# A decoder trunk on one core: TensorE's order through the RWKV scan written out by hand, the small triangular solves moved to GpSimd, and unsplit fp32 weights in the prologue

## The chip, the core and the metric

The kernel runs on one core of a Trainium2 chip. The metric is the device time of one execution, in microseconds (us). TensorE (PE in the profile) does the matrix products, VectorE (DVE) and ScalarE (ACT) work on whole tiles, GpSimd (POOL) can do simple elementwise work, and SyncE (SP) issues DMAs. ACT issues DMAs too, from a queue of its own.

## What is computed

A two-layer decoder trunk over 272 tokens (16 learned ones and 256 given) of width 2048. Layer 0 is RWKV-7 time mixing and a SwiGLU; layer 1 is attention and a SwiGLU. The change is in the time mixing, whose heart is a recurrence over the tokens for 32 heads of 64:

```python
def step(state, inp):
    r_t, d_t, k_t, v_t, kk_t, a_t = inp
    sa = jnp.einsum('bhvk,bhk->bhv', state, -kk_t)
    state = (state * d_t[:, :, None, :]
             + sa[..., None] * (kk_t * a_t)[:, :, None, :]
             + v_t[..., None] * k_t[:, :, None, :])
    return state, jnp.einsum('bhvk,bhk->bhv', state, r_t)
...
y = ((y - mean) * lax.rsqrt(var + GN_EPS)).reshape(b, l, d) * gn_w + gn_b
bonus = (jnp.sum(rh * kh * r_k, axis=-1, keepdims=True) * vh).reshape(b, l, d)
out = ((y + bonus).astype(h.dtype) * g) @ w_o
```

Here r, k and v are projections of mixed neighbouring tokens with 2048 x 2048 weights, and decay, a and the gate g come from narrow two-factor projections (96 and 256 wide, called lora below).

## The kernel before

Activations lie transposed: 16 tiles (k) of 128 channels by 272 tokens. A **dense product** is one 128 x 128 weight block times one such tile. For fp32 accuracy at the faster fp32r rate each weight and activation is split into a high and a low part (ACT casts `whi`, DVE subtracts for `wlo`; the same with `hl` or `hi`/`lo` for activations), and `mm3k` issues three products a block (L191 to L193). So one output block of a projection is 16 x 3 = 48 dense products. A product in raw fp32 needs no split and shows as two records in the trace.

**Prologue** (`prologue`). Tokens are loaded, their squares summed on PE (`ss`), and `rstd_of` gives the norm (Ln, Exp, and four DVE steps, L575 to L578). The first three blocks of w_k are computed together, k outside, as the mixed tiles come (hn L452, u L428, xi L429, hl L254/255); `presplit` splits their weights (L421/422). Then the other 13 blocks follow. Between them the generator `rest` makes the first lora factors (`lr`, raw fp32, L497), g_w1 (split) and the other mixed activations. Each finished block gives the norm of its heads (`kq`, L469).

**Scan** (`pair`, one call for each of 16 pairs of heads). The 256 tokens are cut into 4 chunks of 64, the 16 first ones are a chunk of their own ("0"). A pair needs: zw and za (lora, three products each); v and r (48 dense products each); scaled operands (ARV, BK, AR0, B0, V0); bonus; score products `ba`, `bb` and `b`, masked on DVE into G; products z0 and k0 for chunk 0; transposes `tb` and `tv`, and `vc`, which centres v; the inverse of 40 unit triangular 16 x 16 blocks (**the solver**, L772 to L779, 29 steps on DVE, each of which needs the one before); its extension to 64 x 64 by `yb` and `zb`, twice (s = 16 and 32); `wa`, `rm`; then in bank `cb` the part of the states that needs no earlier state (L896), and four steps (L903), each of which needs S, copied and scaled by ACT from the step before (L905). Then group norm (`vb`), and the gate (`gp`). The solver's blocks go through DRAM to change layout: G is written to s1, the diagonal blocks come back as As, the result Ts goes to s2 and comes back as Tt. All these DMAs are issued on ACT.

What sets the order: pairs are generators, interleaved 13 yields apart (`STRIDE`), with `WAIT1` and `WAIT2` empty yields to cover DMAs; a scheduler then places each engine's instructions by its own estimate of when they are due. At the tail `wo_head` begins four blocks of w_o for 15 of their 16 input tiles (`KHEAD`); `wo_first` (L191 and so on) ends them. FFN and attention follow.

Of the kernel before, what the change touches and what calls it, by code (L numbers as in the profile page):

```python
# [11 lines left out]
F32 = mybir.dt.float32  # L12
# [13 lines left out]
HD = 64  # L26
# [14 lines left out]
L2B = {"da": 1, "g": 2}  # L41
# [3 lines left out]
NSQ = 4  # L45
RSTEP = 7
KR = 8
FRONT = {"zw", "za", "vc", "bonus", "ba", "bb", "z0", "k0", "b00", "b01"}
TAIL = {"wa", "rm0", "rm1", "cb", "vb", "gp"}
WAIT1 = 3  # L50
WAIT2 = 9
STRIDE = 13
PSTEP = 8
NHEAD = 4
KHEAD = 15
ASTRIDE = 2
ASTEP = 4
BUFS = {n: 2 for n in "ARV BK AR0 bv G An Tt pe X BV0 WV0".split()}


def _consts():
# [14 lines left out]
    put("blk", blk)  # L76
    put("blk64", blk / 64)
# [6 lines left out]
    put("mask3", np.concatenate([incl, strict, incl], 1))  # L84
# [20 lines left out]
    first = pos  # L105
    put("onesD", np.full((128, 128), 1.0 / D))
# [17 lines left out]
class Builder:  # L124
# [141 lines left out]
    def build(self):  # L266
        tc, nc = self.tc, self.nc
        with ExitStack() as ctx:
# [6 lines left out]
            nc.scalar.dma_start(self.vecs, self.a["vecs"])  # L275
            self.dvec = {"hdw0": 0, "ha0": NK, "oka": 2 * NK}
            self.dvec.update({f"om{i}": (3 + i) * NK for i in range(6)})
            self.dv = cp.tile([128, 9 * NK + 4], F32, name="dv")
            b = 9 * NK
            nc.vector.memset(self.dv[:, b:b + 1], RMS_EPS)  # L280
            nc.vector.memset(self.dv[:, b + 1:b + 2], GN_EPS)
            nc.vector.memset(self.dv[:, b + 2:b + 3], 1.0)
            self.eps = self.dv[:, b:b + 1]
            self.gneps = self.dv[:, b + 1:b + 2]
            self.one = self.dv[:, b + 2:b + 3]

            def v16(name):
                i = VEC.index(name) * NK
                return self.vecs[:, i:i + NK]

            for dst, src in (("hdw0", "dec_w0"), ("ha0", "a_w0")):
                o = self.dvec[dst]
                nc.vector.tensor_scalar(self.dv[:, o:o + NK], v16(src), 0.5, None, ALU.mult)
            nc.vector.tensor_scalar(self.dv[:, 2 * NK:3 * NK], v16("k_a"), -1.0, 1.0,
                                    ALU.mult, ALU.add)
            nc.vector.tensor_scalar(self.dv[:, 3 * NK:9 * NK], self.vecs[:, 0:6 * NK], -1.0, 1.0,
                                    ALU.mult, ALU.add)
            nv = len(VEC) * NK
            self.kgain = self.vecs[:, nv:nv + 1]
            self.qgain = self.dv[:, b + 3:b + 4]  # L300
            nc.vector.tensor_scalar(self.qgain, self.vecs[:, nv + 1:nv + 2], 128.0 ** -0.5, None,
                                    ALU.mult)
# [34 lines left out]

    def time_mix(self):
# [4 lines left out]
        self.xs2 = self.hid_ctx.enter_context(tc.tile_pool(name="xs2", bufs=2 * NK))  # L343
        self.kp = self.hid_ctx.enter_context(tc.tile_pool(name="kp", bufs=NK))
# [5 lines left out]
        self.fronts = 0  # L350
        with ExitStack() as ctx:
            sp = ctx.enter_context(tc.tile_pool(name="sp", bufs=1))
            self.l2 = ctx.enter_context(tc.tile_pool(name="l2", bufs=2))
# [3 lines left out]
            zero = sp.tile([128, 5, 65], F32, name="zero", tag="P")  # L357
            nc.gpsimd.memset(zero, 0.0)
            for i in range(2):
                st = {}  # L360
                for n, w in (("B0", 64), ("V0", 64), ("SC0", 128)):
# [5 lines left out]
                                  zero.rearrange("p a t -> p (a t)"))  # L367
                self.s2.append(z)
            self.interleave(lambda p: self.pair(p, sp), STRIDE, self.wo_head())
# [4 lines left out]
    def prologue(self, hid):  # L374
# [3 lines left out]
        with ExitStack() as ctx:  # L378
# [3 lines left out]
            hn = [self.xs2.tile([128, T + 1], F32, name="hn", tag="s") for _ in range(NK)]  # L382
            xx = [self.xs2.tile([128, T], F32, name="xx", tag="s") for _ in range(NK)]
            for k in range(NK):
                nc.sync.dma_start(xx[k], a["xT"][:, k, :])
# [14 lines left out]
            rstd = self.rstd_of(ss[:, :T])  # L400


            w0 = [[] for _ in range(G0)]
            raws = []
            n = 0

            def presplit(k0):
                nonlocal raws, n
                if k0 % 8 == 0:
                    raws = []  # L410
                    for m in range(G0):
                        raw = self.wraw.tile([128, 1024], F32, name="raw", tag="raw")
                        nc.sync.dma_start(raw, a["w_k"][m][:, k0 * 128:k0 * 128 + 1024])
                        raws.append(raw)
                for m in range(G0):
                    pool, t = (wx, ("w", "w")) if n < NWX // 2 else (self.whl, ("whi", "wlo"))
                    hi = pool.tile([128, 512], F32R, name="whi", tag=t[0])
                    lo = pool.tile([128, 512], F32R, name="wlo", tag=t[1])
                    n += 1
                    part = raws[m][:, k0 % 8 * 128:k0 % 8 * 128 + 512]  # L420
                    A.copy(hi, part)  # L421
                    V.tensor_tensor(lo, part, hi.bitcast(F32), ALU.subtract)
                    for k in range(4):
                        w0[m].append((hi[:, k * 128:k * 128 + 128], lo[:, k * 128:k * 128 + 128]))
# [21 lines left out]
            for k in range(NK):  # L446
                if k % 4 == 0:
                    presplit(k)
# [752 lines left out]
```

## Time and profile before

| | us |
|---|---|
| median of 3 runs (lowest, highest) | 2740.06 (2737.32, 2741.23) |
| the profiled execution; its span | 2741.77; 2740.0 |
| prologue: start to the scan's first product | 0 to 179.8 |
| scan, to the first dense product of wo_first | 179.8 to 683.2 |
| the rest: wo_first, FFN, attention, FFN | 683.2 to 2740.0 |

The granted TensorE clock was 0.995 over the span. In a row of instructions stand the source line, the engine, the operation, what it writes and reads, and its duration; in a row of groups the count, the busy time, the mean in ns, and the idle time of the engine just before with what ended it. Matmuls are pipelined, so the distance between two starts tells more than a duration.

### The profile page before, as it was taken

The page shows a single profiled execution, that of the slowest core. Times are in us where ns is not written, and L with a number is a line of the kernel's source. Part 1 is how long each engine was busy: PE and PEld are TensorE (multiplying, and loading weights), DVE is VectorE, ACT ScalarE, POOL GpSimd, SP SyncE. Part 2 cuts the span into 40 slices and gives each one's busy share as a digit, 9 for nine tenths or more (in the row PEclk, how much of TensorE's full clock was granted, in tenths as well). Part 3 has the DMA queues.
Part 4 walks back from the last instruction along what each step waited for, and adds up shares of the span by engine and source line. Part 5 has one row for each costly group of instructions (what it writes and reads, how often), then busy time and mean ns, then how long its engine had stood idle before and what let it go on. Part 6 is the DMA issues. An engine that isn't in the chain of part 4 may idle for free.

```text
span 2740.0 us, 53870 instructions
## 1 busy us (share of the span) xinstructions
PE 2689.3 (98%) x20862; PEld 2475.0 (90%) x20862; DVE 1864.8 (68%) x4176; ACT 1493.5 (55%) x3005; POOL 1.2 (0%) x11
## 2 busy tenths in 40 slices
PE   6999999998999999999999999999999999999999
PEld 5888888887999999999999999988888888888888
DVE  7677788786666555555556876577776666666665
ACT  6774555555554444444445764477555455454553
POOL 0000000000000000000000000000000000000000
PEclk9999999999999999999999999999999999999999
DMA  5443333332655555555555555533555665665655
GB/s 169 135 152 100 104 96 103 104 95 83 210 173 168 181 177 167 185 176 162 187 176 167 180 164 169 169 119 105 189 187 179 196 188 180 197 189 179 199 177 179
DMA packets 181279, 439.50 MB, mean 160 GB/s; under 512 B 57984, under 2 KB 84000, under 8 KB 181024
## 3 DMA queue, kind: packets, MB, share of 16 engines
q1 hardware_dynamic: 137632, 428.56, 49.4%
q10 hardware_dynamic: 43392, 7.52, 1.5%
q8 instruction: 163, 2.67, 0.4%
q14 instruction: 92, 0.75, 0.1%
HBM read 430.27 MB, written 5.74 MB: 159 GB/s over the span
## 4 chain that ended last, share of the span: by engine, by line
PE 91%; DVE 3%; DMA 3%; ACT 2%; ACTq 1%; issue 0%; SPq 0%; DVEq 0%
PE mm L197 22%; PE mm L191 16%; PE mm L193 16%; PE mm L192 15%; PE mm L196 11%; DMA raw<-w_k 1%; PE cb L903 1%; PE yb L831 1%; PE rm L871 1%; PE zb L848 1%; PE hms L1038 1%; PE cb L896 1%; PE z L1115 1%; DVE G L721 0%; PE ba L715 0%
## 5 line engine op out<-in xcount | busy, mean ns | idle before, releaser
L173 DVE TENSOR_TENSOR wlo<-raw,whi 128x512 fp32r<-128x512 f32 (+1 forms) x1596 | 1079.0, 679 | 622.3 <-ACT whi L172 598.7
L172 ACT CAST whi<-raw 128x512 fp32r<-128x512 f32 (+1 forms) x1596 | 967.6, 611 | 906.2 <-PE mm L192 577.0
L191 PE MATMUL mm<-hl,whi 128*128 128x272 f32 x3424 | 996.9, 292 | 19.4 <-ACT hl L254 18.5
L193 PE MATMUL mm<-hl,wlo 128*128 128x272 f32 x3424 | 995.9, 291 | 0.0
L192 PE MATMUL mm<-hl,whi 128*128 128x272 f32 x3424 | 991.4, 290 | 0.4 <-DVE hl L255 0.3
L197 PE MATMUL mm<-hl,whi 128*128 128x512 f32 x2624 | 919.8, 395 | 0.0
L196 PE MATMUL mm<-hl,wlo 128*128 128x256 f32 x2624 | 740.6, 282 | 0.0
L191 PEld LDWEIGHTS mm<-hl,whi 128*128 128x128 f32 x3424 | 645.8, 189 | 27.7 <-ACT hl L254 20.5
L192 PEld LDWEIGHTS mm<-hl,whi 128*128 128x128 f32 x3424 | 652.6, 191 | 4.2 <-DVE hl L255 1.3
L193 PEld LDWEIGHTS mm<-hl,wlo 128*128 128x128 f32 x3424 | 647.9, 189 | 4.8 <-issue 1.8
L197 PEld LDWEIGHTS mm<-hl,whi 128*128 128x128 f32 x2624 | 492.5, 188 | 112.7
L196 PEld LDWEIGHTS mm<-hl,wlo 128*128 128x128 f32 x2624 | 494.3, 188 | 0.6
L213 DVE TENSOR_TENSOR h<-h,mm 128x256 f32<-128x256 f32 (+1 forms) x224 | 93.9, 420 | 6.6 <-PE mm L197 6.0
L206 ACT COPY c<-mm 128x256 f32<-128x256 f32 x104 | 38.8, 373 | 79.0 <-PE mm L197 78.9
L191 PE MATMUL mm<-hi,whi 128*128 128x272 f32 x256 | 79.3, 310 | 0.0
L192 PE MATMUL mm<-lo,whi 128*128 128x272 f32 x256 | 77.0, 301 | 0.0
L193 PE MATMUL mm<-hi,wlo 128*128 128x272 f32 x256 | 76.6, 299 | 0.0
L193 PEld LDWEIGHTS mm<-hi,wlo 128*128 128x128 f32 x256 | 48.8, 191 | 2.9 <-issue 2.4
L191 PEld LDWEIGHTS mm<-hi,whi 128*128 128x128 f32 x256 | 48.9, 191 | 2.4
L192 PEld LDWEIGHTS mm<-lo,whi 128*128 128x128 f32 x256 | 48.9, 191 | 1.0
L428 ACT ACTIVATE u<-hn,vecs 128x272 f32<-128x272 f32 x96 | 45.2, 515 | 4.8 <-DVE hn L452 4.8
L1009 ACT ACTIVATE s<-t 128x272 f32<-128x272 f32 (+1 forms) x88 | 37.5, 426 | 18.6 <-DVE t L208 18.5
(275 smaller groups left out, 2158.6 us busy)
## 6 DMA issues: line engine op xcount, KB each, us to landing
raw<-w_gate SPq DMA_DIRECT2D x176, 512.0 KB
raw<-w_up SPq DMA_DIRECT2D x176, 512.0 KB
raw<-w_down SPq DMA_DIRECT2D x128, 512.0 KB
raw<-w_down SPq DMA_DIRECT2D x128, 192.0 KB
raw<-w_k SPq DMA_DIRECT2D x32, 512.0 KB
raw<-w_v SPq DMA_DIRECT2D x32, 512.0 KB
raw<-w_r SPq DMA_DIRECT2D x32, 512.0 KB
raw<-w_o SPq DMA_DIRECT2D x32, 512.0 KB
```

The lines of the kernel that those rows point to most:

```text
L172: nc.scalar.copy(hi, part)
L173: nc.vector.tensor_tensor(lo, part, hi.bitcast(F32), ALU.subtract)
L191: mm(out, w[0], x[0], start=first, stop=False)
L192: mm(out, w[0], x[1], start=False, stop=False)
L193: mm(out, w[1], x[0], start=False, stop=last)
L196: mm(out[:, :n], w[1], x[0], start=first, stop=False, skip_group_check=True)
L197: mm(out, w[0], x[2], start=False, stop=last, skip_group_check=True)
L206: self.nc.scalar.copy(c, out[:, n:])
L213: self.nc.vector.tensor_tensor(h, h, out[:, c:c + n], ALU.add)
L428: A.mul(u, hn[k][:, :T], self.vec(f"mu{i}", k))
L831: PE.matmul(yb[r, i * 64:i * 64 + 64], An[r, i], Tt[r, i], start=True, stop=True)
L1009: nc.scalar.activation(s[:, :n], t[:, :n], AF.Silu)
```

## The change

The generator `pair` becomes a class `Pair` with one method for each step, and `scan` writes the order out: in each round a pair A does its states, steps, norm and gate, the pair behind it (M) the extension of the inverse, `wa` and `rm`, the next (B) its scores, bonus, transposes and solver, and the last (C) its lora. `f(n)` takes n steps of three dense products from `stream`, which runs through v and r of all pairs and then w_o. On PE this order is final; the scheduler still orders the other engines.

With it: the solver is on GpSimd, as are the memsets of P and the copies to pe. bonus and vb are sums of a high and a low part in fp32r with one block matrix (`head_sums`). `vc` is gone; the centring is a factor in the products of tv and z0. Norms take three DVE steps after Exp. Small products take their banks in rotation over six (`rbank`). Some tiles get other buffer counts. In the prologue the first three w_k blocks, the lora factors and g_w1 are raw fp32 products; kq is kept and written out in two halves; tokens are loaded from two queues. w_o is begun with 12 tiles in place of 15.

```diff
-KHEAD = 15
+KHEAD = 12
...
-            self.interleave(lambda p: self.pair(p, sp), STRIDE, self.wo_head())
...
+            with tc.manual_schedule(engines={mybir.EngineType.PE}):
+                self.scan(sp)
...
-            rstd = self.rstd_of(ss[:, :T])
...
-                    A.copy(hi, part)
-                    V.tensor_tensor(lo, part, hi.bitcast(F32), ALU.subtract)
...
+            V.tensor_tensor(rn, r, r, ALU.mult)
+            V.scalar_tensor_tensor(rn, ms, RMS_EPS, rn, ALU.add, ALU.mult)
+            V.scalar_tensor_tensor(rn, rn, -3.0, r, ALU.add, ALU.mult)
...
+            w0 = {}
+            for m in range(G0):
+                raw = self.wraw.tile([128, 1024], F32, name="raw", tag="raw")
+                nc.sync.dma_start(raw, a["w_k"][m][:, :1024])
+                w0[m, 0], w0[m, 1] = raw[:, :512], raw[:, 512:]
+            for j in (2, 3):
+                for m in range(G0):
+                    w0[m, j] = wx.tile([128, 512], F32, name="raw", tag="w")
+                    nc.sync.dma_start(w0[m, j], a["w_k"][m][:, j * 512:j * 512 + 512])
...
+                    o = k % 4 * 128
+                    nc.tensor.matmul(ps[m][:, :T], w0[m, k // 4][:, o:o + 128], x,
+                                     start=k == 0, stop=k == NK - 1)
+                xk.append(self.split(x, x0))
...
+                names = ((1, ["dec_w1"]), (4, ["a_w1"]), (5, ["g_w1", "g_w1"]))
...
+        for n in range(-3, NK):
+            get = lambda i: pairs.get(n + i)
+            A, M, B, C = get(0), get(1), get(2), get(3)
+            f = fill if C else lambda k: fill(k / 2)
+            if A:
+                A.states()
+                A.step(1)
+            if B:
+                B.chunk0()
+            if A:
+                A.step(2)
+            if B:
+                B.scores(0)
+            if A:
+                A.step(3)
+            if B:
+                B.scores(1)
+            if A:
+                A.step(4)
+            if B:
+                B.neg()
+                B.bonus()
+            f(2)
+            if B:
+                B.tokens()
+            if C:
+                C.lora()
+            f(3 + (LEAD if n == -3 else 0))
+            if A:
+                A.norm()
+                f(1)
+                A.gate()
+                f(3)
...
+            if M:
+                M.left(16)
+            if B:
+                B.values()
+                B.solve()
+                if n + 2 == NK - 1:
+                    self.rot = self.rot[1:]
+            f(4)
+            for g in ("right", 16), ("left", 32), ("right", 32), ("apply", None), ("trans", None):
+                if M:
+                    getattr(M, g[0])(*g[1:] if g[1] else ())
+                f(3 if g[0] == "trans" else 4)
+
...
+    def rbank(self, name):
+        self.turn[1] += 1
+        pool, tag = self.rot[self.turn[1] % len(self.rot)]
+        return pool.tile([128, 512], F32, name=name, tag=tag)
...
+        for k in range(KHEAD):
+            self.o.append(self.split(self.oraw[k], self.xs1))
...
+
+        out = self.b.rbank(name)[:, :T]
+        self.PE.matmul(out, block, x[0], start=True, stop=False)
+        self.PE.matmul(out, block, x[1], start=False, stop=True)
+        return out
...
+        s1 = b.dram.tile([10, 65, 64], F32, name="s1", tag="s1")
+        for r in range(2):
+            b.dq.dma_start(s1.rearrange("(a r) i t -> r i a t", r=2)[r, 0:64, 0:4],
+                           G[HS[r], r, :, 2])
+            b.dq.dma_start(s1[8 + r, 0:64], self.SC0[HS[r], 0:64])
+        self.As = b.sp.tile([40, 16, 16], F32, name="As", tag="As")
+        b.dq.dma_start(self.As, self.diag(s1))
...
+    def solve(self):
+
+        b, V, As = self.b, self.nc.gpsimd, self.As
+        Ts = b.sp.tile([40, 16, 16], F32, name="Ts", tag="Ts")
+        Tm = b.sp.tile([40, 64], F32, name="Tm", tag="Tm")
+        V.tensor_tensor(Ts.rearrange("p i t -> p (i t)"), As.rearrange("p i t -> p (i t)"),
+                        b.cst("eye16")[:40], ALU.add)
+        for i in range(1, 15):
+            n = 15 - i
+            t = Tm[:, :i * n].rearrange("p (i t) -> p i t", t=n)
+            V.tensor_tensor(t, Ts[:, 0:i, i:i + 1].to_broadcast([40, i, n]),
+                            As[:, i:i + 1, i + 1:].to_broadcast([40, i, n]), ALU.mult)
+            V.tensor_tensor(Ts[:, 0:i, i + 1:], Ts[:, 0:i, i + 1:], t, ALU.add)
+        s2 = b.s2[self.p % 2]
+        b.dq.dma_start(self.diag(s2), Ts)
+        self.Tt = self.big("Tt", 5, 64)
+        for r in range(2):
+            b.dq.dma_start(self.Tt[HS[r]], s2.rearrange("(a r) i t -> r i a t", r=2)[r, 0:64])
...
+                PE.matmul(tv[HS[r], u:u + 128], self.ARV[:, c, 1], b.cst("ident"), start=True, stop=True)
+                PE.matmul(tv[HS[1 - r], u:u + 128], self.ARV[:, c, 2], b.cst("cen"), start=True, stop=True)
...
```

On TensorE, here is the place in the steady state where the state steps begin, before (cb are the states, mm a projection; whi and wlo are weights):

```order
L896 MATMUL cb<-G,X 64x64 x4
L903 MATMUL cb<-S,Mp 64x64 x2
L903 MATMUL cb<-Rh,S 64x64 x2
L192 MATMUL mm<-lo,whi 128x272
L193 MATMUL mm<-hi,wlo 128x272
L191 MATMUL mm<-hi,whi 128x272
L192 MATMUL mm<-lo,whi 128x272
L193 MATMUL mm<-hi,wlo 128x272
L903 MATMUL cb<-S,Mp 64x64 [waits DVE_49,Activation_49]
L903 MATMUL cb<-S,Mp 64x64
L903 MATMUL cb<-Rh,S 64x64 x2
L191 MATMUL mm<-hi,whi 128x272
```

And after:

```order
L1247 MATMUL cb<-G,X 64x64 x4
L1255 MATMUL cb<-S,Mp 64x64 [waits DVE_49]
L1255 MATMUL cb<-S,Mp 64x64
L1255 MATMUL cb<-Rh,S 64x64 [waits DVE_49]
L1255 MATMUL cb<-Rh,S 64x64
L1043 MATMUL z_6266<-AR_5931,B_1_2016 64x32 [waits PE_49]
L1043 MATMUL z_6266<-AR_5931,B_1_2016 64x32
L1046 MATMUL z_6266<-consts,B_1_2016 64x64 x2
L1048 MATMUL z_6266<-consts,V_1_2018 64x64 x2
L1255 MATMUL cb<-S,Mp 64x64 [waits DVE_49,Activation_49]
L1255 MATMUL cb<-S,Mp 64x64
L1255 MATMUL cb<-Rh,S 64x64 [waits DVE_49]
```

The dense products between two steps are gone; the z products of another pair stand there, so that states, steps, z, scores and b make one run. The second step waits for ACT's copy of S, as it did.

On ACT, where the solver's result is sent off, before (rs is a norm's intermediate, s_1 is s2 and s_7844 is s1 in DRAM, w2's halves are cast into gh):

```order
L918 ACT_TABLE_LOAD
L918 ACTIVATE rs_7820<-vb,dv 128x272 [waits PE_49]
L780 DMA s_1_2283<-Ts 40x16x16 [waits DVE_49]
L620 CAST gh<-w_7499 128x256 [waits PE_49]
L919 ACT_TABLE_LOAD
L919 ACTIVATE rs_7820<-rs_7820 128x272 [waits Activation_49]
L754 DMA s_7844<-G 64x4x64 [waits DVE_49]
L754 DMA s_7844<-G 64x4x64 [waits DMAHW6_49,DVE_49]
L783 DMA Tt<-s_1_2283 64x5x64 [waits DMAHW7_49,DMAHW3_49]
L783 DMA Tt<-s_1_2283 64x5x64 [waits DMAHW0_49]
```

And after:

```order
L1118 DMA s_0_2014<-Ts 40x16x16 [waits Pool_49]
L936 CAST dah<-w_7294 128x256
L167 CAST whi<-raw 128x512 [waits DMAHW6_49,PE_49]
L936 CAST gh<-w_7376 128x256 [waits DMAHW4_49]
L1187 ACTIVATE S<-yb,pe 128x64 [waits DVE_49]
L167 CAST whi<-raw 128x512 [waits PE_49]
L1121 DMA Tt<-s_0_2014 64x5x64 [waits DMAHW5_49]
L1121 DMA Tt<-s_0_2014 64x5x64
L167 CAST whi<-raw 128x512 [waits DMAHW6_49,PE_49]
L167 CAST whi<-raw 128x512 [waits PE_49,Activation_49]
L1211 COPY X<-wa 64x2x128 [waits DVE_49]
L1211 COPY X<-wa 64x2x128
```

The DMA of Ts waited for DVE; it now waits for GpSimd, and weight casts, a copy to S, the DMAs of Tt and the copies X<-wa come behind it.

On DVE, where rm's results are added, before (Ts and Tm are the solver's):

```order
L777 TENSOR_TENSOR Tm<-Ts,As 40x50 [waits DVE_49]
L875 TENSOR_TENSOR Rh<-rm_7180,ARV 128x2x64 [waits PE_49]
L779 TENSOR_TENSOR Ts<-Ts,Tm 40x5x10 [waits DVE_49]
L877 TENSOR_TENSOR Mp<-rm_7180,consts 128x2x64
L777 TENSOR_TENSOR Tm<-Ts,As 40x54 [waits DVE_49]
L686 SCALAR_TENSOR_TENSOR ARV<-kk,P 128x4x64
L779 TENSOR_TENSOR Ts<-Ts,Tm 40x6x9 [waits DVE_49]
L688 TENSOR_TENSOR kk<-ta,kk 128x272 [waits DVE_49]
```

And after:

```order
L1209 COPY Ah<-wa 128x256 [waits DVE_49,PE_49]
L1170 STREAM_TRANSPOSE Tn<-Tt 128x256 [waits DMAHW7_49,DMAHW1_49]
L168 TENSOR_TENSOR wlo<-raw,whi 128x512 [waits PE_49,Activation_49]
L1225 TENSOR_TENSOR Mp<-rm_7157,consts 128x2x64 [waits PE_49]
L1032 TENSOR_TENSOR AR_6867<-rs,P 128x16 [waits Activation_49]
L1033 TENSOR_TENSOR ARV<-rs,P 128x4x64
L1227 TENSOR_TENSOR Rh<-rm_7157,ARV 128x2x64
L1035 SCALAR_TENSOR_TENSOR rs<-rs,vecs,k_6860 128x272 [waits DVE_49]
L1225 TENSOR_TENSOR Mp<-rm_7158,consts 128x2x64 [waits PE_49]
L1227 TENSOR_TENSOR Rh<-rm_7158,ARV 128x2x64
```

The solver's steps are gone from between these, and the transpose Tn, which waits for the DMAs of the next pair's Tt, comes ahead of Mp and Rh.

More of the change, by code (lines that the diff above doesn't have):

```diff
@@ L44 @@
 NWX = 10
[L45 to L52, printed above, removed]
+NSQ = 3
+RSTEP = 4
+NXL = 7
+LEAD = 4
 PSTEP = 8
 NHEAD = 4
-KHEAD = 15
+KHEAD = 12
 ASTRIDE = 2
 ASTEP = 4
-BUFS = {n: 2 for n in "ARV BK AR0 bv G An Tt pe X BV0 WV0".split()}
+BUFS = {n: 2 for n in "BK AR0 G An Tt X BV0".split()}
+BUFS.update(ARV=3, bv=3, pe=4)
 def _consts():
@@ L105, in _consts @@
     first = pos
+    put("blk", blk)
     put("onesD", np.full((128, 128), 1.0 / D))
@@ L274, in build @@
             self.vecs = cp.tile([128, NV], F32, name="vecs")
[L275 to L302, printed above, removed]
+            self.dv = cp.tile([128, 12 * NK + 5], F32, name="dv")
             self.rstd_p = ctx.enter_context(tc.tile_pool(name="rstd", bufs=1))
@@ L381, in prologue @@
             pt = ctx.enter_context(tc.tile_pool(name="pt", bufs=3))
[L382 to L385, printed above, removed]
+            hn, xx = self.hn, self.xx
             self.pre0 = tc.keep_in_program_order(
```

871 lines of the change are left out of this document (457 added, 414 removed).

## Prediction

> **What bounds the kernel now.** I read the page first, for the busy shares and the chain that ended last.
>
> ```profile
> PE 2689.3 (98%) x20862; PEld 2475.0 (90%) x20862; DVE 1864.8 (68%) x4176; ACT 1493.5 (55%) x3005; POOL 1.2 (0%) x11
> PE 91%; DVE 3%; DMA 3%; ACT 2%; ACTq 1%; issue 0%; SPq 0%; DVEq 0%
> ```
>
> TensorE is busy for 98% of the span and is 91% of the chain. So time goes only where PE gets fewer or denser products, or where its few waits go. GpSimd does nothing. Next the stretches, in the table of busy times by window (us, then PE, PEld, DVE, ACT, POOL busy, granted clock, DMA share, GB/s).
>
> ```profile
> 21.23:53.43 32.20, 26.43 (x151) 24.16 (x151) 26.96 (x61) 21.21 (x51) 0.00 (x0) 0.90 0.44 139
> 53.43:178.10 124.67, 122.22 (x859) 108.22 (x858) 91.98 (x195) 100.05 (x228) 0.99 (x7) 1.00 0.45 144
> 178.10:683.20 505.10, 483.54 (x5736) 414.29 (x5734) 388.21 (x1389) 278.51 (x666) 0.00 (x0) 0.99 0.35 100
> 428.60:457.70 29.10, 28.58 (x352) 24.39 (x351) 23.40 (x86) 16.68 (x40) 0.00 (x0) 1.00 0.36 102
> 900.00:1200.00 300.00, 300.00 (x2396) 300.00 (x2395) 172.05 (x295) 135.00 (x235) 0.00 (x0) 1.00 0.57 179
> 683.20:2740.00 2056.80, 2052.00 (x14114) 1926.37 (x14114) 1346.09 (x2485) 1081.07 (x2037) 0.00 (x0) 1.00 0.56 176
> ```
>
> The first two rows are the prologue (first dense stage, then the rest), the third the scan, the fourth one pair of it in the steady state. From 683 us on the change touches nothing but 36 products of wo_first. The dense row gives the unit: 300 us / 2396 = **0.1252 us a dense product**. A pair of the scan holds 96 of these and 12 like them (zw, za, gp): 108 × 0.1252 = 13.5 of 29.1 us. The other 15.6 is small products, the price of switching to and from them, and a wait. The switching price stands in PE's timeline (start, duration, instruction):
>
> ```profile
> 443.01 0.29 PE L884 MATMUL cb<-SC,WV 64*64 64x16 f32 x4
> 443.40 0.29 PE L896 MATMUL cb<-G,X 128*64 128x64 f32 x4
> 443.51 0.29 PE L896 MATMUL cb<-X,G 128*64 128x64 f32 x4
> 444.20 0.33 PE L903 MATMUL cb<-S,Mp 64*64 64x64 f32 x4
> 444.36 0.28 PE L903 MATMUL cb<-Rh,S 64*64 64x64 f32 x4
> 444.57 0.40 PE L191 MATMUL mm<-hi,whi 128*128 128x272 f32 x1
> 444.81 0.29 PE L192 MATMUL mm<-lo,whi 128*128 128x272 f32 x1
> 445.07 0.28 PE L191 MATMUL mm<-hi,whi 128*128 128x272 f32 x1
> 445.29 0.33 PE L903 MATMUL cb<-S,Mp 64*64 64x64 f32 x4
> ```
>
> Inside a run four records of 64 columns follow each other in 0.11 (443.40 to 443.51). The last four before a dense product take 0.21 (444.36 to 444.57), the first dense one 0.24 instead of 0.125, and the last dense one before the next run 0.22. That is 0.10 + 0.115 + 0.095, about **0.30 us for each run**. Written out, before has 13 such runs a pair. One wait is left:
>
> ```profile
> L766 PE MATMUL b<-BK,ARV 64*64 64x64 f32 x16 | 0.5, 230 | 0.5 <-DVE bv L729 0.5
> ```
>
> So 29.1 = 13.5 dense + 13 × 0.30 + 0.5 wait + **11.2 of small products**.
>
> **The change, part by part: PE in the scan.** The new order keeps 8 runs a pair. Bonus and vb become two dense-like products each, so 112 × 0.1252 = 14.0. Switching is 8 × 0.30 = 2.4. The three fp32 products of 272 columns (vc, bonus, vb) leave the small ones. Such a product takes two records, and its pace is read from lr:
>
> ```profile
> 70.80 1.99 PE L497 MATMUL lr<-xi,raw 128*96 128x272 f32 x8
> ```
>
> (1.99 − 0.39, the length of a record) / 7 = 0.229, so 0.457 a product and 1.4 for three. The tv products turn from four transposes into eight true products of 128 columns, two at a time in half the array: by the same pace 8 × 0.215 / 2 = 0.86, some 0.4 more than now. Small products: 11.2 − 1.4 + 0.4 = 10.2.
>
> What is late next is the copy of S, which each state step waits for. Up to now dense products stand between the steps.
>
> ```profile
> 444.69 0.32 ACT L905 ACTIVATE S<-cb,pe 128x64 f32<-128x64 f32 x1 [0.81 <-PE cb L903]
> ```
>
> The step began at 444.20, the copy ends at 445.01: 0.81, and some 0.05 to hand over. In the new order z, or half of the scores, stands between: the step's own 0.24 and about 0.42. That leaves 0.2 bare, three times: 0.6. In sum **P = 14.0 + 2.4 + 10.2 + 0.6 = 27.2 us a pair**. I put it at 26.2 (S hidden, runs that share an entry) to 28.2 (0.1 bare wait more at each run).
>
> Over the scan: before, 1716 dense products (16 × 96 and 180 of w_o) are 214.8, and 16 × (29.1 − 12.0) = 273.6; the 16.7 left of 505.1 is filling and draining. After, 1680 are 210.3; 16 × (27.2 − 12.0) = 243.2; I keep the 16.7, and add 36 × 0.125 = 4.5 that move to wo_first. That is 474.7, a gain of **30.4**.
>
> **The solver on GpSimd.** On DVE its 29 steps (L772, L777, L779) lay between other work:
>
> ```profile
> 437.37 0.41 DVE L772 TENSOR_TENSOR Ts<-As,consts 40x256 f32<-40x256 f32 x1
> 445.85 0.21 DVE L777 TENSOR_TENSOR Tm<-Ts,As 40x54 f32<-40x54 f32 x1
> 446.09 0.21 DVE L779 TENSOR_TENSOR Ts<-Ts,Tm 40x54 f32<-40x54 f32 x1
> 451.00 0.17 DVE L779 TENSOR_TENSOR Ts<-Ts,Tm 40x14 f32<-40x14 f32 x1
> ```
>
> That was 13.8 us elapsed (437.37 to 451.17), but two steps with nothing between are 0.24 apart, so alone it would be 28 × 0.24 + 0.4 = 7.1. DVE loses 5.7 us (28 × 0.19 + 0.4) of 23.4 a pair; neither it nor ACT, 16.7, was the bound, so that is worth nothing by itself. GpSimd has shown no such operation. The nearest rows are memsets on both engines:
>
> ```profile
> L363 POOL MEMSET SC<- 128x128 f32 x2 | 0.4, 205 | 0.0
> L1193 POOL MEMSET const-float32-0.0<- 128x1 f32 x1 | 0.1, 99 | 0.2 <-issue 0.2
> L389 DVE MEMSET od<- 128x128 f32 x1 | 0.2, 165 | 0.0
> L644 DVE MEMSET P<- 128x1 f32 x16 | 0.9, 59 | 0.1
> ```
>
> 205/165 = 1.24 at 128 columns, 99/59 = 1.68 at one. The steps have 14 to 56, so the time S of a solve is 8.8 to 11.9; I take the middle, **10.3**. The difference is 40 ns at both widths, which would make 7.1 + 29 × 0.04 = 8.3; 7.1 itself, DVE's own pace, is the lowest end. A shorter solve gains nothing more, since it is hidden then.
>
> What decides is the loop that S stands in, through ACT's queue, which issues these DMAs in order:
>
> ```profile
> 451.20 0.28 ACTq L780 DMA_DIRECT2D s<-Ts  x1
> 453.17 0.63 ACTq L754 DMA_DIRECT2D s<-G  x1
> 454.64 0.60 ACTq L783 DMA_DIRECT2D Tt<-s  x1
> 446.84 0.62 ACT L172 CAST whi<-raw 128x512 fp32r<-128x512 f32 x1 [0.75 <-PE mm L192]
> L863 ACT COPY X<-wa 64x256 f32<-64x256 f32 x2 | 0.7, 367 | 0.1
> 453.00:453.50 0.50, 0.50 (x7) 0.50 (x5) 0.50 (x3) 0.41 (x1) 0.00 (x0) 1.00 0.50 52
> 453.50:454.00 0.50, 0.50 (x5) 0.36 (x3) 0.50 (x2) 0.49 (x1) 0.00 (x0) 1.00 0.00 0
> L173 DVE TENSOR_TENSOR wlo<-raw,whi 128x512 fp32r<-128x512 f32 x8 | 5.5, 681 | 1.1 <-ACT whi L172 1.0
> ```
>
> The DMA engines fall idle by 453.5, so s2, issued at 451.20, took about 2.2 to land. From the states of a pair (T0): 1.6 for states and step 1 (443.01 to 444.57), 1.25 for z and the scores (44 records' worth of 0.028), 0.9 for steps 2 and 3 with their waits, then two masks of 512 columns at 0.68: 5.1. The G DMAs, 0.63 each, start after the first mask and are issued at about 6.0 and landed at 8.2; As needs 0.3 and 1.9 more: the solver starts at T0 + 10.4. After it: s2's issue 0.3 and landing 2.2, two Tt issues 1.2, two weight casts 1.2, two copies X<-wa 0.7. Only then can the next states start. All of this is queued on ACT behind the wait for GpSimd, the weight casts that PE's dense products need too; on DVE, Tn waits for Tt ahead of wlo, Mp and Rh. So **P is at least 10.4 + S + 5.6 = 16 + S**. With S = 10.3 this is 26.3, below 27.2: hidden, with 0.9 to spare. From S = 11.2 on it is the bound, and each us costs 13 us (13 full iterations).
>
> The Trainium skill's GPSIMD Engine Reference, "Elementwise — side-by-side cycle accounting", speaks against this part: it states 4497 ns against 2293 ns for an fp32 tensor_tensor of 2048 elements, 1.96 times DVE's. By that S would be an estimated 13.9 and P 29.9, in place of 10.3 and 27.2; the memset rows agree that GpSimd is slower, but by 1.24 to 1.68.
>
> **The prologue.** Before, 48 × 3 dense products, 18.0 at 0.125, took 32.2, since casts and subtractions of weights stood with those of the activations on DVE and ACT. After, 48 fp32 products at 0.457 are 21.9, and DVE has hn, xi and hl left for each k, less than PE's 1.37. The granted clock of 0.90 in the first row costs 10% of the stage, about 3, in both: 24.9, so 7.3 less. In front of it stand these:
>
> ```profile
> 16.65 0.44 DVE L576 SCALAR_TENSOR_TENSOR rstdt<-ss,rstdt 128x272 f32<-128x272 f32 x1
> 17.99 0.29 DVE L577 TENSOR_SCALAR rstdt<-rstdt 128x272 f32<-128x272 f32 x1
> 20.77 0.40 ACT L254 CAST hl<-xi 128x272 fp32r<-128x272 f32 x1
> 21.23 1.05 PE L191 MATMUL mm<-hl,whi 128*128 128x272 f32 x3 [6.72 <-ACT hl L254]
> ```
>
> The 0.9 before L577 (a weight subtraction got in between), its own 0.3 and the 0.46 from hl's cast to the first product go: 1.7. Behind the stage lr grows from 32 to 64 fp32 products (+14.6) and g_w1's 96 dense ones go (−12.0): 2.6 more. The 2.4 of idle PE in the second row partly go with g_w1's splits: 2. In sum 7.3 + 1.7 − 2.6 + 2 = **8.4**, with ends at 4 (those stalls stay and the stage waits for DVE) and 14 (no clock loss, no idle). The x tokens over two queues count nothing: they move at the DMA engines' pace, not at issue's.
>
> **The sum.** The profiled execution is 2741.8 (span 2740.0), 1.7 above the median of 2740.1. 2741.8 − 30.4 − 8.4 = 2703.0; less 1.7 for the median, **2701**.
>
> **The rivals.**
> - *GpSimd's chain takes PE's place*, S from 11.2 to 13.8. For it: 11.9 by the smallest memset, and the loop has only 0.9 to spare. Against: the steps have more columns than one. P 27.2 to 29.8, so 2701 to 2735.
> - *The gain is just eaten*, S from 13.8 to 14.6. 39 us of gain / 13 is 3.0 us of P: 2735 to 2745. The mechanism is a step's pace of 0.46 to 0.49 in place of 0.24: two operands to read where a memset has none. The ratio of the GPSIMD Engine Reference in the Trainium skill would end here, at 2736.
> - *Slower: DVE and GpSimd hold each other up.* Each solver step waits for the one before, so a hold of 0.2 to 0.3 at 28 steps, half the length of a DVE operation of 0.44 to 0.68 found in progress, makes 6 to 8 of the 10.3 more: S = 16 to 18, P = 32 to 34, 2763 to 2790. It decides from S = 14.6 on. For it: DVE is busy 23.4 of 29.1, with wlo alone 5.5 at 0.68 each, two inputs from SBUF. Against: the trace has no moment with both engines at work, so it can't show it. The Trainium skill's SBUF — State Buffer, "Who interferes with whom", states that a DVE instruction with two SBUF inputs contends with a GpSimd one that reads SBUF; no run here shows that yet.
> - *The order doesn't do what it says*: runs joined, but with bare waits in them (Ys behind the norm chain on DVE, S behind the s1 issues on ACT). At 0.3 for each of the five runs saved, P = 28.7: 2725.
>
> **How the numbers follow.** Forecast (2685 to 2717 by P's own bounds): 0.48. Chain or bare waits, but still faster: 0.25. Just eaten: 0.10. Slower by contention: 0.17. A measurement here can tell 0.2%, 5.5 us, from no change: faster 0.73, same 0.10, slower 0.17. The range goes from 2675 (P = 26.2 and 14 in the prologue, with a little of the fill gone) to 2745, the end of "just eaten"; some 0.15 lies above and 0.04 below.
>
> **What would show it.** Right: the states recur every 27.2 us; GpSimd's first and last solver step lie 10 to 11 us apart; PE's only repeated wait is for S, 0.2 each; the first w_k stage lasts 25 us. Wrong: PE idle in front of the states with ACT X named, or in front of Mp's step with DVE named (the chain binds); solver steps of 0.5 us and more (contention); waits for Ys or hl inside the runs (bare waits). What would make the number wrong most cheaply is S: 1 us beyond 11.2 is 13 us.

## The result, and the profile after

The change made the kernel slower: median **2808.43 us** (4 runs, 2805.9 to 2810.86) against 2739.38 for the kernel before (4 runs, 2737.32 to 2741.23), a ratio of 1.0253 with a 95% interval of [1.0237, 1.0269]. That is 69 us more, where 39 less were forecast. The profiled execution's span is 2809.0.

First the page of the kernel after: busy times, and the shares of the chain that ended last.

```profile
PE 2688.8 (96%) x20942; PEld 2484.5 (88%) x20942; DVE 1797.5 (64%) x3586; ACT 1489.9 (53%) x3005; POOL 178.8 (6%) x539
PE 83%; POOL 6%; DMA 4%; ACT 2%; DVE 2%; issue 2%; ACTq 1%; POOLq 0%; DVEq 0%; SPq 0%
```

PE's share of the chain fell from 91% to 83%, and GpSimd, which had none, has 6%. The next rows show where in the program. They are from PE's timeline of both kernels (start, duration, instruction): the first and the last of the 16 state products of the scan, before (L884), then after (L1240).

```profile
242.82 0.29 PE L884 MATMUL cb<-SC,WV 64*64 64x16 f32 x4
...
670.32 0.29 PE L884 MATMUL cb<-SC,WV 64*64 64x16 f32 x4
```

```profile
253.85 0.29 PE L1240 MATMUL cb<-SC,WV 64*64 64x16 f32 x4
...
730.23 0.29 PE L1240 MATMUL cb<-SC,WV 64*64 64x16 f32 x4
```

From first to last states the kernel took 427.5 and takes 476.4: +48.9. In front of the scan 3.6 came on (its first product starts at 183.40 instead of 179.82, rows below); from there to the first states 7.4 (70.45 against 63.00); behind the last states 9.1 (2078.8 against 2069.7). Together 69.0. So 56 of the 69 us lie in the scan up to its last states, where the forecast's working had 35 less (30.4, and the 4.5 it moved behind them).

The steady pair comes every 32 to 34 us (once 35.9) instead of 27.2. Busy times by window (us, then PE, PEld, DVE, ACT, POOL, granted clock, DMA share, GB/s): one pair, from states to states, and the stretch in it that follows PE's wait.

```profile
417.73:451.21 33.48, 28.94 (x361) 25.69 (x360) 20.91 (x54) 17.29 (x43) 10.80 (x33) 0.91 0.32 89
447.80:454.00 6.20, 6.20 (x71) 5.46 (x73) 3.60 (x11) 2.16 (x6) 0.14 (x2) 0.50 0.40 131
```

PE is idle for 4.5 of the 33.5 us, and part of its busy time runs at a granted clock of 0.50. What it waits for stands in the waits of that pair (engine, line and the releaser: us in total, times, longest):

```profile
ACT dah L936 <- POOL Ts L1116: 5.7, 1, 5.7
...
PE rm L1221 <- DVE Ah L1209: 4.0, 1, 4.0
```

The chain of the same pair (start, us, what) shows how the one leads to the other:

```profile
417.80 0.33 PE cb L1240 x4
...
422.86 1.27 DVE G L1071 x2
...
424.81 2.73 DMA s<-G
...
427.78 1.91 DMA As<-s
...
429.85 0.91 POOL Ts L1109
...
442.29 2.38 DMA s<-Ts
...
444.69 0.60 ACTq L1121
...
445.33 0.64 ACTq L1121
...
446.06 0.63 ACT whi L167
...
446.71 0.04 DVE wlo L168
446.75 0.57 issue
447.32 0.43 DVE Ah L1209
...
447.80 1.15 PE rm L1221 x16
```

This is the loop of the forecast, link for link as far as the Tt issues, but longer in each of its three parts. From the states to the solver's start: 12.1 (417.73 to 429.85). The solve: 12.4 (to 442.29). From there to the next states: 8.9 (to 451.21). Behind the two Tt issues there is no data that rm needs from Tt: a weight cast on ACT and a weight subtraction on DVE merely stand in their queues in front of Ah, which rm does need. From the third pair on PE waits for Ah in front of rm in eleven pairs running, 3.2 to 6.3 us each time.

### The profile page after: what moved, and what is told of

Read it like the earlier page. It is cut to its first block, busy times and chain, and to the rows that moved or that the text cites. A ratio compares the mean times of both kernels' runs of the same rounds, so it can differ in the third digit from the quotient of the medians.

```text
span 2809.0 us, 54126 instructions
## 1 busy us (share of the span) xinstructions
PE 2688.8 (96%) x20942; PEld 2484.5 (88%) x20942; DVE 1797.5 (64%) x3586; ACT 1489.9 (53%) x3005; POOL 178.8 (6%) x539
## 4 chain that ended last, share of the span: by engine, by line
PE 83%; POOL 6%; DMA 4%; ACT 2%; DVE 2%; issue 2%; ACTq 1%; POOLq 0%; DVEq 0%; SPq 0%
PE mm L192 22%; PE mm L186 14%; PE mm L188 14%; PE mm L187 14%; PE mm L191 11%; POOL Ts L1116 3%; POOL Tm L1114 3%; PE lr L540 1%; DMA As<-s 1%; DMA s<-Ts 1%; DMA raw<-w_k 1%; ACT whi L167 1%; PE cb L1255 1%; DMA s<-G 1%; PE hms L791 1%
## 5 line engine op out<-in xcount | busy, mean ns | idle before, releaser
L186 PE MATMUL mm<-hl,whi 128*128 128x272 f32 x3344 | 982.2, 294 | 6.8 <-ACT whi L167 5.1
L188 PE MATMUL mm<-hl,wlo 128*128 128x272 f32 x3344 | 973.7, 291 | 4.0 <-DVE wlo L168 4.0
L187 PE MATMUL mm<-hl,whi 128*128 128x272 f32 x3344 | 971.0, 290 | 0.0
L186 PEld LDWEIGHTS mm<-hl,whi 128*128 128x128 f32 x3344 | 636.6, 190 | 19.0 <-issue 8.6
L187 PEld LDWEIGHTS mm<-hl,whi 128*128 128x128 f32 x3344 | 643.1, 192 | 0.6
L192 PEld LDWEIGHTS mm<-hl,whi 128*128 128x128 f32 x2624 | 492.5, 188 | 113.0
L1116 POOL TENSOR_TENSOR Ts<-Ts,Tm 40x14 f32<-40x14 f32 (+6 forms) x224 | 77.7, 347 | 17.5
L1114 POOL TENSOR_TENSOR Tm<-Ts,As 40x14 f32<-40x14 f32 (+6 forms) x224 | 75.5, 337 | 17.5
L1221 PE MATMUL rm<-G,Ah 64*64 64x128 f32 x256 | 16.0, 383 | 43.8 <-DVE Ah L1209 43.8
L1221 PEld LDWEIGHTS rm<-G,Ah 64*64 64x64 f32 x256 | 10.4, 186 | 47.1 <-DVE Ah L1209 46.4
```

The source lines that it names most:

```text
L186: mm(out, w[0], x[0], start=first, stop=False)
L187: mm(out, w[0], x[1], start=False, stop=False)
L188: mm(out, w[1], x[0], start=False, stop=last)
L192: mm(out, w[0], x[2], start=False, stop=last, skip_group_check=True)
L1114: V.tensor_tensor(t, Ts[:, 0:i, i:i + 1].to_broadcast([40, i, n]), As[:, i:i + 1, i + 1:].to_broadcast([40, i, n]), ALU.mult)
L1116: V.tensor_tensor(Ts[:, 0:i, i + 1:], Ts[:, 0:i, i + 1:], t, ALU.add)
```

## The experiments

**Is it the solver's engine?** The theory was that GpSimd's solve, held up by DVE, is too long for the loop; the rival, that the new order of TensorE waits for itself. First the solve goes back to DVE.

```diff
-        b, V, As = self.b, self.nc.gpsimd, self.As
+        b, V, As = self.b, self.nc.vector, self.As
```

> The solver goes back to VectorE, all else as in the changed kernel. Theory 1 (the loop over GpSimd's solve and ACT's in-order queue sets the 33 us a pair): ACT no longer stands 5.7 us before the cast of dah, PE no longer waits 4 us for Ah in front of rm, its clock stays at 1.0, a pair takes 27 to 28 us, the time is 2715 to 2740 us. Theory 2 (the written order itself costs it, by bare waits inside the joined runs): a pair stays above 32 us, the time above 2795 us.

Measured: 2779.2, ratio 1.0153 [1.0138, 1.0168]. That is 29 us less than after, yet slower than before; neither theory's number. The pairs are uneven: some last 27 us, some 30, others 34 to 36. In a slow one ACT's timeline (start, us, instruction, idle before) shows the Tt issues standing in front of copies:

```profile
433.16 0.28 ACTq L1118 DMA_DIRECT2D s<-Ts  x1
...
436.78 1.25 ACTq L1121 DMA_DIRECT2D Tt<-s  x2
438.07 0.27 ACT L1053 COPY BV<-z 128x128 f32<-128x128 f32 x1 [2.38 <-issue]
438.24 0.32 ACT L1257 ACTIVATE S<-cb,pe 128x64 f32<-128x64 f32 x1
```

On the chain s2's transfer takes 3.6 us (433.16 to 436.78), and the Tt issues wait for it. ACT does no work for 2.38 us there, 1.25 of which are the two issues; the copy to S stands behind them, and PE idles 1.77 for it in front of its next step. So GpSimd isn't the whole story; a wait in ACT's queue costs time with either solver.

**Half of the solve.** Seven of the fourteen steps are left out, so the solution is incomplete.

```diff
-        for i in range(1, 15):
+        for i in range(1, 8):
```

> Leaves out the second half of the solve: 7 of 14 columns, 14 of its 28 steps; the DMAs stay on ACT. S falls from 12.4 to 6 to 7 us. Theory 1: the period follows S until PE bounds it: 27 to 28 us a pair, 2715 to 2740 us. Theory 2: 32 to 33 us a pair, 2800 us or more.

One execution: 2733.85 beside a median of 2737.7 before; a solve takes some 6.5 us, a steady pair 27.0 to 28.2. With a short solve the written order reaches nearly its forecast pace.

**Only the solver, in the kernel before.** The three operations of L772, L777 and L779 go to GpSimd; nothing else changes.

```diff
-        V.tensor_tensor(Ts.rearrange("p i t -> p (i t)"), As.rearrange("p i t -> p (i t)"),
+        nc.gpsimd.tensor_tensor(Ts.rearrange("p i t -> p (i t)"), As.rearrange("p i t -> p (i t)"),
...
-            V.tensor_tensor(Ts[:, 0:i, i + 1:], Ts[:, 0:i, i + 1:], t, ALU.add)
+            nc.gpsimd.tensor_tensor(Ts[:, 0:i, i + 1:], Ts[:, 0:i, i + 1:], t, ALU.add)
```

> The kernel before with one thing changed: its solver on GpSimd. Theory 1: the scheduler takes the solve for shorter than it is, and puts the DMA of Ts and those of Tt ahead of the copies to S and of weight casts on ACT, so a pair takes longer than 29.05: 30 to 33 us, 2750 to 2800 us. If a solve on GpSimd does no harm in an order that isn't written out: 2730 to 2745 us.

Measured: 2840.43, ratio 1.0372 [1.0355, 1.0389], 35 to 37 us a pair. In the old order this part alone costs 102 us; the kernel after, which has the rest of the change as well, is 32 us faster than that. The waits of four pairs:

```profile
ACT whi L172 <- POOL Ts L779: 19.2, 4, 4.8
...
PE vc L695 <- ACT v L661: 14.4, 4, 3.6
```

The same picture: ACT's weight cast stands behind the Ts DMA's wait for GpSimd, 4.8 us a pair, and PE waits 3.6 for what ACT does later.

**Another queue for the solver's DMAs.** If only ACT's queue is the fault, GpSimd's own queue cures it.

```diff
-        b.dq.dma_start(self.diag(s2), Ts)
+        b.nc.gpsimd.dma_start(self.diag(s2), Ts)
...
-            b.dq.dma_start(self.Tt[HS[r]], s2.rearrange("(a r) i t -> r i a t", r=2)[r, 0:64])
+            b.nc.gpsimd.dma_start(self.Tt[HS[r]], s2.rearrange("(a r) i t -> r i a t", r=2)[r, 0:64])
```

> The solver stays on GpSimd, 12.4 us long; only the DMAs of its result (Ts to s2, s2 to Tt) are issued from GpSimd's own queue, so that nothing on ACT waits for it. Theory 1 in its form that the queue is what hurts: a pair takes 27 to 29 us, the time is 2715 to 2750 us. Theory 3 (the length of the solve hurts by the data alone, whatever queue carries it): 32 to 33 us a pair, no change from 2808. Theory 2: no change either.

Measured: 2854.74, ratio 1.0425 [1.0407, 1.0442]; 35 to 38 us a pair, a miss. ACT is free, but s2 takes longer from that queue: 3.1 to 5.9 us over the 16 pairs, median 4.5. From ACT's queue in the kernel after, the Tt issue, which waits for s2 to land, follows the Ts issue within 2.0 to 5.1, median 2.1. Two of the longer transfers on the chain:

```profile
458.76 5.54 DMA s<-Ts
...
496.22 3.77 DMA s<-Ts
```

The waits of three pairs show what stands behind it on another engine:

```profile
DVE Tn L1170 <- DMA Tt<-s: 26.3, 3, 9.5
...
PE cb L1255 <- DVE Mp L1225: 19.2, 3, 7.2
```

Tn, the transpose that waits for Tt, stands on DVE ahead of Mp, which PE's steps wait for. The solve is longer here too, about 15 us in most pairs instead of 12 to 13. SP's queue was not tried.

**Moving what waits, not the solver.** The result of a solve isn't read until a later phase of its pair, so its DMAs can be issued later. In the first version the Ts DMA goes behind the copies X<-wa, the Tt DMAs into the next round behind An, and Tn behind the masks G:

```diff
+    def send(self, after):
+        b = self.b
+        with b.tc.issue_after(after.ins) if after else ExitStack():
+            b.dq.dma_start(self.diag(b.s2[self.p % 2]), self.Ts)
...
-        V.transpose(self.Tn.rearrange(flat), Tt[:, :4].rearrange(flat))
+        with b.tc.issue_after(b.last_g.ins):
+            V.transpose(self.Tn.rearrange(flat), Tt[:, :4].rearrange(flat))
```

> The solver stays on GpSimd and the DMAs on ACT's queue, but they are issued later: Ts to s2 behind the copies X<-wa of the round, s2 to Tt in the next round behind the copies An; on VectorE the transpose Tn of the next pair's Tt stands behind the masks on G. Theory 1, as the second queue showed (what hurts is what stands in order behind the wait, on ACT and on VectorE): no wait for Ah in front of rm, none for Mp in the steps, 27 to 28 us a pair, 2720 to 2750 us. Theory 3 (the data's own way from scores to Tt is too long): 32 us a pair or more, 2800 or more.

Measured: 2823.72, ratio 1.0308 [1.0292, 1.0323]: a miss. The wait of PE for Ah is gone, but a new one has come (waits of three pairs):

```profile
DVE Tn L1186 <- DMA Tt<-s: 12.2, 3, 4.5
...
PE vb L956 <- DVE lo L949: 8.5, 2, 4.6
```

Tt now lands later, and Tn stands in front of sq's low part, which vb multiplies. It has two variants. With only Tn moved:

> Only the transpose Tn is put behind the masks on G; the DMAs are where the change has them. Theory 1 with ACT's queue as the main path: ACT still stands until the solve ends, with dah, the weight casts and X<-wa behind it; a pair stays at 31 to 33 us, 2780 to 2808 us. If VectorE's Tn were the main path: below 30 us a pair, below 2770 us.

One execution: 2809.83, as after; ACT's dah still waits 5.4 us a pair for GpSimd and PE's rm up to 4.1 for Ah. With all of the first version and the x tokens on one queue:

> As the run with both waits moved, and the token tiles loaded from SP's queue alone: 5 us less than that run, 2715 to 2745 us. By theory 3: 2795 or more.

Measured: 2820.16, ratio 1.0296 [1.028, 1.0311]; its interval overlaps that of the version with both queues.

**No wait at all.** This kernel sends As in place of Ts, so the solution is left out of the result; GpSimd still solves, and nobody waits for it.

```diff
-        b.dq.dma_start(self.diag(s2), Ts)
+        b.dq.dma_start(self.diag(s2), As)
```

> GpSimd still runs the whole solve, but what goes to s2 is its input As, so nothing waits for it; the solution is left out of the result. Everything else, DMAs on ACT included, stays. Theory 1 (the wait for the solve, with what stands behind it, sets the period): 27 to 28 us a pair, 2720 to 2745 us, as with half a solve. Theory 4 (GpSimd's and VectorE's hold on each other, not the wait, is what slows the scan): 30 us a pair or more, above 2770 us.

Measured: **2715.4**, ratio 0.9914 [0.9899, 0.9929]. The window of a pair:

```profile
459.80:486.84 27.04, 26.48 (x362) 23.62 (x361) 20.28 (x51) 17.38 (x42) 11.62 (x33) 1.00 0.39 111
```

27.04 us at full clock, with the whole GpSimd load beside it (its solves take 13.3 us on average). Then the same without the solve's instructions:

> As the run in which nothing waits for the solve, and GpSimd doesn't run it either (the solution is left out). What is left between the two is what GpSimd's steps and VectorE's operations cost each other. Theory 1: VectorE has room, so no more than 3 us: 2712 to 2717 us. Theory 4: 10 us or more, below 2706 us.

Measured: 2712.04, ratio 0.9893 [0.9876, 0.9909]. A steady pair takes 26.7. The 3.4 us between the two are about all that GpSimd's work costs the others when nobody waits for it, and the intervals overlap.

**All waits moved far enough.** GpSimd solves in full. As in the first version the Ts DMA stands behind X<-wa; the Tt DMAs go behind the cast of sq in the next round, Tn behind sq's low part, and sq is split right after step 4; the x tokens are on SP.

```diff
-        V.transpose(self.Tn.rearrange(flat), Tt[:, :4].rearrange(flat))
+        with b.tc.issue_after(b.last_lo.ins):
+            V.transpose(self.Tn.rearrange(flat), Tt[:, :4].rearrange(flat))
...
         self.b.dump("y", self.p, self.y)
+        self.sqx = self.high_low(self.sq)
```

> Solver on GpSimd, tokens from SP's queue, the Ts DMA behind the copies X<-wa, the Tt DMAs in the next round behind the cast of sq, Tn behind sq's low part; sq is split right after the last step. The earlier run with both waits moved only exchanged PE's wait for Ah (4.0 us) for one for sq's low part (4.6). If that was the last thing behind the wait: 28 us a pair, 2710 to 2740 us. If the round has no place for a solve of 12.4 us and its four DMA hops: 32 us or more, 2790 or more.

Measured: **2728.67**, ratio 0.9963 [0.9949, 0.9977]: faster than both kernels, though only 0.4% faster than before. Of these 10 us the tokens' queue alone may be 4 to 5: it made 3.6 us between the two versions above, and 5 in the last experiment. The window of a pair, then GpSimd's timeline from the first to the last operation of a solve in the steady state:

```profile
409.57:436.73 27.16, 26.42 (x362) 23.61 (x361) 19.45 (x51) 16.77 (x43) 11.79 (x33) 1.00 0.37 110
```

```profile
448.40 0.73 POOL L1113 TENSOR_TENSOR Ts<-As,consts 40x256 f32<-40x256 f32 x1 [12.75 <-DMA As<-s]
...
462.25 0.44 POOL L1120 TENSOR_TENSOR Ts<-Ts,Tm 40x14 f32<-40x14 f32 x1
```

This solve takes 14.3 us (448.40 to 462.69), longer than the 12.4 of after (most here take 13.0 to 13.7), and a pair still lasts 27.2. So a round has room for the data's own way from the scores to Tt, which the first version's 2823.72 had left open. With the solver on DVE in the same order:

> The same with the solver on VectorE. If the DMAs' place on ACT made the uneven 27 and 34 us of the run with the solver on VectorE: 28 us in each round, 2700 to 2735 us. If VectorE's solver steps between other work are too slow for the written order: 30 us or more, 2750 or more.

Measured: 2768.11, ratio 1.0107 [1.0092, 1.0123], steadily 30.6 a pair. There the solve stands in DVE's own queue in front of what PE needs; the waits of three pairs:

```profile
DVE Tn L1186 <- DMA Tt<-s: 13.1, 3, 4.9
...
PE zb L1209 <- DVE Tm L1118: 5.7, 3, 1.9
```

So in this order GpSimd is the better engine, by 39 us, though each of its steps is slower.

**The tokens.** One line of after is undone:

```diff
-            (nc.sync, nc.scalar)[k % 2].dma_start(self.xx[k], self.a["xT"][:, k, :])
+            nc.sync.dma_start(self.xx[k], self.a["xT"][:, k, :])
```

> All 16 token tiles are loaded from SP's queue as before the change; nothing else. If ACT's first square (at 8.8 us, before the change 3.5) waits because ACT itself is busy issuing eight of the loads: it starts at 3.5 to 4 us, the first w_k product comes at 19 to 20 us in place of 24.3, and the time falls by 4 us to about 2804. If the DMA engines set it: no change.

One execution: 2803.27, 5 below the median of after, whose fastest run was 2805.9. What it shows of the prologue stands below.

## Why the prediction was wrong

**TensorE's own part was right.** Forecast: 27.2 us a pair, and 30.4 less over the scan with what lies behind it. The kernel without the wait has 27.04 a pair; from the scan's first product it needs 60.3 to the first states, 392.0 to the last and 2078.55 to the end, where before needs 63.0, 427.5 and 2069.7: −2.7 − 35.5 + 8.9 = −29.3. In that sum the tail grew by 8.9 instead of the 4.5 of the moved products; what the other 4.4 are, no run took apart. Nor were the terms of 27.2 measured one by one: the sum came out, and the only waits that PE shows in that pair are 0.2 for Ys and 0.2 for G.

**The step that failed** is "P is at least 10.4 + S + 5.6 = 16 + S. With S = 10.3 this is 26.3, below 27.2: hidden". It is the right loop with all three terms too small. Measured in one pair: 12.1 + 12.4 + 8.9 = 33.4. By their sizes:

- *8.9 instead of 5.6.* I let the states follow directly on the copies X<-wa. In fact Ah stands in between, behind a weight cast on ACT and its subtraction on DVE (chain, 446.06 to 447.75), and then rm (1.15) and nine dense products. All of it runs slowly, since PE has been idle for 4.0 us (its wait for Ah, above). In the 6.2 us behind that wait the granted clock is 0.50, and a dense product takes 0.23 to the start of the next instead of 0.125. Nine take 2.3 instead of 1.1. In the version with all waits moved PE is idle for only 0.7 us of a pair (26.42 busy of 27.16), and the pair's clock is 1.00. The Trainium skill's "TensorE: Matmul & The Clock Gate", Part 1, states that after an idle window of about 3.4 us the array gets half its clock, until about 3.4 us of sustained work; the trace agrees on the 4.0 us of idle time and on the 0.50. The clock stays at 0.50 for 6.8 us in some pairs of this scan (447.27 to 454.08) and for 3.4 in others (481.41 to 484.80, behind an idle time of 3.24, a little less than that window).

- *12.1 instead of 10.4.* States and step 1 run slowly as well; PE's timeline has 2.4 us from their start to the next product, where I had 1.6:

```profile
417.73 0.40 PE L1240 MATMUL cb<-SC,WV 64*64 64x16 f32 x4
...
420.11 0.25 PE L1043 MATMUL z<-AR,B 64*64 64x32 f32 x4
```

  The G transfer takes 2.73 on the chain, and I had 2.2. Together that is 1.3 of the 1.7.

- *12.4 instead of 10.3.* The step's own length came out, the hold was not counted. GpSimd's and DVE's timelines side by side, two stretches of the solve each:

```profile
433.81 0.27 POOL L1114 TENSOR_TENSOR Tm<-Ts,As 40x50 f32<-40x50 f32 x1
434.16 0.53 POOL L1116 TENSOR_TENSOR Ts<-Ts,Tm 40x50 f32<-40x50 f32 x1
...
439.49 0.59 POOL L1114 TENSOR_TENSOR Tm<-Ts,As 40x44 f32<-40x44 f32 x1
440.15 0.27 POOL L1116 TENSOR_TENSOR Ts<-Ts,Tm 40x44 f32<-40x44 f32 x1
```

```profile
434.11 0.44 DVE L1273 TENSOR_TENSOR sq<-rs 128x272 f32<-128x272 f32 x1 [1.33 <-ACT rs L1272]
...
438.50 1.46 DVE L168 TENSOR_TENSOR wlo<-raw,whi 128x512 fp32r<-128x512 f32 x2
```

  The step at 434.16 meets sq, the square of an SBUF tile with itself, and takes 0.53; its neighbour of the same width takes 0.27. The step at 439.49 meets wlo: 0.59, and its successor 0.27. Worked out from both timelines over all 16 solves: the steps that overlap no DVE operation (154 of 448) take 0.21 at 14 columns to 0.29 at 56; the 19 that meet only a wlo take 0.26 more on average, the four of them that began ahead of the wlo no more than 0.002, the 15 that began while it ran 0.32 to 0.36; the steps that meet only DVE operations with one input from PSUM take no more than 0.006 extra. At the unheld lengths a solve takes 10.2, the forecast's figure; but that was the middle of a bracket of 8.8 to 11.9 from memsets, so how close it came is luck. The Trainium skill's "SBUF — State Buffer", "Who interferes with whom", states that GpSimd's ports are DVE's second pair, under an exclusive lock; the trace agrees, and gives the size of a hold here, 0.32 to 0.36 where the DVE operation was first. The "1.96 times" of the Trainium skill's GPSIMD Engine Reference, "Elementwise — side-by-side cycle accounting", isn't borne out at these widths: an unheld step's start to the next one's is 0.29 to 0.36, DVE's was 0.24.

The rival "slower: DVE and GpSimd hold each other up" gave the right side and a right pair (32 to 34), but not by its sizes: it wanted S = 16 to 18, and S is 12.4; its 2763 to 2790 us lie below the 2808 measured. What I set against it, that the trace has no moment with both engines at work, is not so: GpSimd's memsets of 173.72 to 174.70 stand beside a wlo of 174.06 to 174.73. Memsets read nothing, so they say little of two engines that read; but the 205 ns that priced GpSimd at 128 columns came from there. The hold is 2.2 of the 6.3 us that a pair exceeds the forecast's 27.2 by. And the kernel without the wait and the one with all waits moved, in which the solver is held as much or more (13.3 and 13.6 us a solve on average, 12.7 in after), show that the hold costs next to nothing once nobody waits. **What the solve's length costs is decided by the instructions queued behind its result.** My bound took that queue as given and used it only as a sum to compare with 27.2. It had 0.9 us of margin under three terms of which none was read from a row of the new order; errors of 1.7, 2.1 and 3.3 went through it in full.

**The prologue**: forecast −8.4, measured +3.6. ACT's timeline after, and its first square before:

```profile
1.69 7.02 ACTq L312 DMA_DIRECT2D xx<-xT  x7
8.76 0.75 ACT L413 ACTIVATE sq<-xx 128x272 f32<-128x272 f32 x2 [5.82 <-DMA xx<-xT]
```

```profile
3.50 0.97 ACT L394 ACTIVATE sq<-xx 128x272 f32<-128x272 f32 x2 [1.02 <-DMA xx<-xT]
```

I counted the tokens over two queues as nothing, since they move "at the DMA engines' pace". But ACT issues half of them itself, 7.0 us of it, and only then squares the first: 5.3 later. With the tokens on SP alone the first square starts at 3.66, the first w_k product at 20.78 instead of 24.31, and the one execution is 5 us faster. In front of the first stage the forecast was −1.7 and 3.1 came on (24.31 against 21.23). The stage itself took 25.5, close to the forecast's 24.9:

```profile
24.31:49.80 25.49, 23.79 (x97) 19.22 (x97) 22.63 (x53) 18.17 (x44) 0.00 (x0) 1.00 0.37 121
```

That is luck: it runs at a clock of 1.00, where I had taken a tenth off, so my 21.9 without that loss was 3.6 too short; 1.7 of these are PE idle at its end, waiting for kt from ACT. The rest of the prologue took 126.39 before, to the scan's first product (53.43 to 179.82), so the forecast is 127.0 (+ 2.6 − 2); it took 133.6 (49.80 to 183.40). Of that 5.40 is idle time at its end, where PE waits for dah from ACT; before this was 1.45:

```profile
183.40 0.59 PE L186 MATMUL zw<-dec_w1h,dah 96*128 96x272 f32 x1 [5.40 <-ACT dah L936]
```

```profile
179.82 0.39 PE L191 MATMUL zw<-dec_w1h,dah 96*128 96x272 f32 x1 [1.45 <-ACT dah L620]
```

Five waits of kq for ACT's xi make another 5.7 us, where before three waits of kq make 2.3. So PE's idle time there, which I let shrink by 2, grew from 3.9 to 11.2. The parts give the whole: +3.1, −6.7 (25.5 against 32.2) and +7.2 are +3.6.

**What the moved version leaves.** Its median is 13 us above that of the kernel without the wait, its profiled span 17.8 (2731.4 against 2713.6). The first states start at 245.73 and 243.06, +2.7; the twelve steady pairs take 27.3 on average instead of 27.1, +2.9; the last three pairs take 77.4 against 67.1, +10.3. So most of it lies in the draining of the pipeline, where PE has less other work to set against the waits. Another placing there was not tried.

## What to carry over

Before work moves to a slower, idle engine, list what stands behind the wait for its result on every in-order queue, the DMA issues of a compute engine included. How long the idle engine took mattered most where work stood behind its result: there half a solve was worth some 75 us. With the same full solve on the same engine the kernel took 2820.16 us or 2728.67 (both with the tokens on SP), according to where the solve's last transfers, their one reader and the split of sq stood. A bound with 0.9 us of margin that is multiplied by 13 is no bound until each of its terms stands on a row, and a wait long enough to let TensorE's clock fall costs a second time after it.

## What was not expected of the hardware

A GpSimd step that begins while DVE is at a wlo, which has two SBUF inputs, grows by 0.32 to 0.36; one that begins ahead of it doesn't. The DVE operation can grow too. DVE's timeline has this one beside GpSimd's first operation of a solve (429.85 to 430.75). Three of the 16 of them take 0.98 to 0.99, the other 13 take 0.43 to 0.45; the group:

```profile
430.07 0.99 DVE L988 TENSOR_TENSOR k<-k,kt 128x272 f32<-128x272 f32 x1
```

```profile
L988 DVE TENSOR_TENSOR k<-k,kt 128x272 f32<-128x272 f32 x16 | 8.7, 542 | 0.0
```

The s2 transfers issued from GpSimd's queue took 3.1 to 5.9 us, median 4.5; with ACT's queue in the kernel after the Tt issue behind them came within 2.0 to 5.1, median 2.1. And a DMA issue on ACT that waits holds every later ACT operation, 5.7 us in the pair shown.
